# A transformer layer's residual stream moved into the output tensor by accumulating DMAs, its norm squares applied one sum later, and its down projection taken in three groups

## The chip, the cores and the metric

The kernel runs on one core of a Trainium2 chip. The metric is the device time of one execution in microseconds. The figure for a kernel is the median of its runs; beside it stands one profiled execution, whose trace is read here.

## What is computed

One layer of a streaming encoder on 640 tokens of width 2048 (512 of a prompt, 8 x 16 of samples). Only its second half matters here:

```python
merged = concatenate([rms_norm(attn, g_attn_out), rms_norm(ssm, g_ssm_out)])
h = x + merged @ w_out                                      # 2048 x 2048
f = rms_norm(h, g_ffn)
h = h + (silu(f @ w_gate) * (f @ w_up)) @ w_down            # 2048 x 5632, 5632 x 2048
gate = sigmoid(rms_norm(h, g_ple) @ w_ple_gate)             # 2048 x 2048
h = h + gate * (p_i @ w_ple_proj)
```

All in float32. The gate's other factor, `p_i @ w_ple_proj`, is computed earlier and lies in memory (`pj_dr`).

## The kernel before, in words

Activations are kept transposed: features on the partitions, tokens along the free axis, so a "pair" is two blocks of 128 features by 640 tokens (640 KB). After attention and the state-space part (up to about 780 us) come five stages of the same make: the output projection (cells `o`, 8 of them), the gate and up projections (`g` and `u`, 22 each), the down projection (`d`) and the gate for the layer input (`p`, 8). A cell multiplies weights by activations into one pair of output features. It does so by a Strassen-Winograd scheme: seven products of half-size blocks instead of eight, each into a PSUM bank of its own.

**Weight units.** A cell eats "units" of 512 KB: weights of 512 input features by 256 output features. `Ring` streams them: `load` (L53) has SP fetch a unit, two ahead; `split` (L67) has DVE form four sums (L109 to L112), ACT round the seven blocks to the short form (`wh`, L86) and DVE take the remainder (`wl`, L87). There are two buffers of each. A unit is 42 matmuls: seven products, two blocks of 128 input features, three terms (L1231 to L1233: high by high, high by low, low by high).

**Activation tiles.** The input of a stage stands in SBUF as tiles of 1120 KB a pair: the seven Winograd blocks. They are written to memory in that form (`fc_dr`, `tc_dr`, `hc_dr`; `keep`, L1193), fetched by SP (`fetch`, L1205) into one of eight places, and cut in two halves in place (`whole`, `cut`, L1075: ACT rounds, L1076; DVE subtracts, L1077). `fetch` issues the cut right behind the load, but for a few tiles that `cut_late` handles.

**A cell's end.** `strassen` (L1252) empties the seven banks: two copies on ACT (L1258, L1260), six adds on DVE (L1259 to L1265), one on POOL (L1266). Buffers for pairs rotate over two (`pair`, L1169).

**Behind an `o` cell** (L1303 to L1317): SP loads the pair of `x`; DVE adds it (L1306); ACT scales by the norm's weight into `c` (L1293); DVE forms the Winograd sums of `c` (L118 to L121); SP stores `c` and stores the sum to `h_dr` (L1316); ACT squares (L1275) and DVE adds the squares to the running sum (L1279, L1280). The norm's factor itself is applied behind the next stage's products (`by_rows`, L1282), once `scale_rows` has made it from the sum of squares.

**The down projection** has 44 blocks of 128 input features, that is 22 tiles or 11 units, for each of the 8 pairs of output, and only eight places. So `down_cells` (L129) visits each pair several times with some of the units: two groups of four pairs, 28 visits. A visit that isn't the last sends its sum to `h_dr` by an accumulating DMA from POOL (L1372). At the last visit SP loads what has been gathered (`hx`), DVE adds it (L1376), and scaling, Winograd sums, squares follow as above; the sum goes to `h2_dr`.

**The last stage** multiplies the sigmoid by `pj`, loads the pair of `h2_dr` (`hy`), adds it on POOL (L1399) and stores the output by SP (L1400). Its eighth cell is written out by hand so that little is left behind the last matmul.

The order of the instructions on each engine is not that of the text: a planner that the program uses at build time lays them out, with the text's order as preference. Each engine then goes through its own list in order.

Of the kernel before, what the change touches and what calls it, by code (L numbers as in the profile page):

```python
# [9 lines left out]
F32 = mybir.dt.float32  # L10
# [4 lines left out]
OP = mybir.AluOpType  # L15
# [113 lines left out]
def down_cells():  # L129

    low, high = range(4), range(4, 8)
    steps = [(low, 0, 2), (high, 0, 4), (low, 2, 6), (high, 4, 8), (low, 6, 8), (high, 8, 11), (low, 8, 11)]
    return [(j, range(a, b), a == 0, b == FT // 4) for js, a, b in steps for j in js]

# [28 lines left out]
def hybrid_step(ctx: ExitStack, tc: tile.TileContext, io):  # L165
# [21 lines left out]
    cells = down_cells()  # L187
    units += [(1, io["w_down"][j, u]) for j, us, _, _ in cells for u in us]
    units += [(1, io["w_pg"][j, u]) for j in range(8) for u in (2, 3, 0, 1)]
    ring = Ring(nc, stp, units)  # L190
# [5 lines left out]
    m_dr = dp.tile([D, NTOK], F32, name="m_dr")  # L196
    h_dr = dp.tile([D, NTOK], F32, name="h_dr")
    h2_dr = dp.tile([D, NTOK], F32, name="h2_dr")
    tc_dr = dp.tile([FT // 2, P, 7, NH2], F32, name="tc_dr")
# [732 lines left out]
    def attention(h):  # L932
# [133 lines left out]
    def scale_group(s, name):  # L1066
# [3 lines left out]
                  gp_.tile([P, NTOK], F32, tag="sq", name="rz" + name, bufs=2))  # L1070

    def rows(dram, j):
        return dram[2 * j * P : 2 * (j + 1) * P, :].rearrange("(a p) n -> p a n", p=P)

# [127 lines left out]

    later = {}

    def fetch(name, slot, dram, i, late=False):  # L1205
        k = kp_tile("k" + name, slot)
        x = k[:, 1].bitcast(F32)
        nc.sync.dma_start(x, dram[i])
        if late:
            later.setdefault(i // 2 - 2, []).append(lambda: whole(k, x))  # L1210
            return k
        return whole(k, x)

    def cut_late(u):
        for f in later.pop(u, ()):
            with tc.issue_after(ring.done[0]), tc.issue_after(ring.done[1]):
                f()

    def products(name, kps, after=None, order=None):
# [53 lines left out]

    def squares(s, x, t, first, other=nc.vector):
        nc.scalar.activation(t, x, AF.Square)  # L1275
        if first:
            nc.vector.tensor_tensor(s, t[:, 0], t[:, 1], op=OP.add)
        else:
            nc.vector.tensor_tensor(s, s, t[:, 0], op=OP.add)  # L1279
            other.tensor_tensor(s, s, t[:, 1], op=OP.add)  # L1280

# [12 lines left out]

    fk = []
    for j in range(8):
        after = None
        if j == 7:
            def after(u):
                for i in (2 * u, 2 * u + 1):  # L1300
                    if i < 7:
                        fk.append(fetch(f"f{i}", i, fc_dr, i, late=i == 6))
        r = strassen(f"o{j}", mk, after)  # L1303
        x = pair(f"x{j}")
        nc.sync.dma_start(x, io["xT"][2 * j : 2 * j + 2].rearrange("a p n -> p a n"))
        nc.vector.tensor_tensor(r, r, x, op=OP.add)  # L1306
        c = seven(f"c{j}")
        scaled(c, r, gffn, j)
        if j < 7:
            keep(nc.vector, c, fc_dr, j)  # L1310
        else:
            winograd_rows(nc.vector, c[:, :4], c[:, 4:])
            kf7 = kp_tile("kf7", 7)
            fk.append(kf7)
            later.setdefault(1, []).append(lambda: whole(kf7, c))
        nc.sync.dma_start(rows(h_dr, j), r)  # L1316
        squares(ssqh, r, x, j == 0)  # L1317

# [9 lines left out]
    for f in range(FT // 2):  # L1328
        z = strassen(f"g{f}", fk, cut_late if f == 0 else None)
# [18 lines left out]
    for j, us, _, _ in cells:  # L1348
        for u in us:
            uses[u] = uses.get(u, 0) + 1  # L1350
    hk, hslot = {}, {4: 6, 5: 7, 6: 0, 7: 1, 0: 2, 1: 3, 2: 4, 3: 5}
    ready = []

    def next_h():
        i = ready.pop(0)
        hk[i] = fetch(f"h{i}", hslot[i], hc_dr, i)

    for n, (j, us, first, last) in enumerate(cells):
        def after(i, us=us, n=n):
            uses[us[i]] -= 1  # L1360
            if not uses[us[i]] and n < len(cells) - 4:
                next_t()
            if n < 2 and i:
                next_t()
            if n == len(cells) - 1:
                for _ in range(min(2, 3 - i)):
                    if ready:
                        next_h()
# [7 lines left out]
        nc.vector.tensor_tensor(r, r, x, op=OP.add)  # L1376
        c = seven(f"hc{j}")
        scaled(c, r, gple, j)
        if j in (3, 4, 5):
            winograd_rows(nc.vector, c[:, :4], c[:, 4:])  # L1380
            hk[j] = whole(kp_tile(f"kh{j}", hslot[j]), c)
        else:
            keep(nc.vector, c, hc_dr, j)
            ready.append(j)
        nc.sync.dma_start(rows(h2_dr, j), r)
        squares(ssqp, r, x, j == 4)
    hk = [hk[i] for i in (4, 5, 6, 7, 0, 1, 2, 3)]
    for j in range(7):
        z = strassen(f"p{j}", hk)
        if j == 0:  # L1390
# [14 lines left out]
    nc.sync.dma_start(x, rows(pj_dr, 7))  # L1405
    nc.sync.dma_start(y, rows(h2_dr, 7))
    ps = products("p7", hk, order=(1, 2, 6, 5, 3, 7, 4))
# [145 lines left out]
```

## Time and profile before

| | |
|---|---|
| median of 3 runs | 2935.68 us (2934.81 to 2939.37) |
| the profiled execution, its own time | 2942.17 us |
| its span, first to last instruction | 2940.4 us |
| granted TensorE clock, mean | 0.984 |
| PE busy | 2828.1 us (96%) |
| DVE busy | 2241.3 us (76%) |
| ACT busy | 1241.2 us (42%) |
| POOL busy | 360.3 us (12%) |
| DMA | 449.16 MB, mean 153 GB/s |

PE is TensorE, DVE VectorE, ACT ScalarE, POOL GpSimd, SP SyncE. A wait is put down to the instruction that ended it. Busy time of PE is from the start of a matmul to its modelled end; matmuls overlap, so the count of matmuls in a stretch says more than the busy share.

### The profile page before, as it was taken

What the parts mean: (1) busy time and instruction counts of PE and PEld (TensorE: products, weight loads), DVE (VectorE), ACT (ScalarE), POOL (GpSimd) and SP (SyncE); (2) the same over time, 40 slices, a digit from 0 to 9 for tenths busy, and PEclk for the clock granted to TensorE, in tenths of its full rate; (3) what the DMA queues carried; (4) which work ended last, traced back from release to release, by engine and by line L of the source; (5) the groups of instructions that cost most, each with busy time, mean ns of one, the idle gap of its engine ahead of it and who ended that gap; (6) DMA issues with size and microseconds to landing.
All of it is one profiled execution on the core that took longest, in us unless ns stands there. A gap on an engine that the chain in (4) does not pass through costs nothing. (4 is left out here: it accounts for less than half of the span.)

```text
span 2940.4 us, 47366 instructions
## 1 busy us (share of the span) xinstructions
PE 2828.1 (96%) x19051; PEld 2716.3 (92%) x19051; DVE 2241.3 (76%) x3629; ACT 1241.2 (42%) x1628; POOL 360.3 (12%) x405
## 2 busy tenths in 40 slices
PE   8999999999889889999999999999999999999998
PEld 6889988887789889999999999999999999998898
DVE  7758254445688888888888888888887777899888
ACT  5343355556644453333333333333433344345433
POOL 1213300001000001101111111111110110100011
PEclk9999999999999999999999999999999999999999
DMA  5666734546545623232323333333555455647444
GB/s 174 168 187 179 244 118 169 182 156 239 205 141 180 240 98 125 95 124 96 119 101 118 102 118 102 118 102 118 205 145 148 135 158 170 164 158 273 136 158 140
DMA packets 137484, 449.16 MB, mean 153 GB/s; under 512 B 14096, under 2 KB 34672, under 8 KB 124464
## 3 DMA queue, kind: packets, MB, share of 16 engines
q1 hardware_dynamic: 120032, 396.47, 39.9%
q0 software_dynamic: 15936, 45.47, 6.1%
q10 hardware_dynamic: 1296, 4.20, 0.4%
q8 instruction: 149, 2.44, 0.3%
q14 instruction: 71, 0.58, 0.1%
HBM read 342.25 MB, written 101.18 MB: 151 GB/s over the span
## 5 line engine op out<-in xcount | busy, mean ns | idle before, releaser
L86 ACT ACTIVATE wh<-wst 128x768 fp32r<-128x768 f32 x328 | 276.9, 845 | 660.0 <-issue 320.0
L87 DVE TENSOR_TENSOR wl<-ws,wh 128x1024 fp32r<-128x1024 f32 x328 | 423.6, 1291 | 102.1 <-ACT wh L86 101.7
L86 ACT ACTIVATE wh<-ws 128x1024 fp32r<-128x1024 f32 x328 | 344.6, 1051 | 358.0 <-DVE ws L112 357.9
L87 DVE TENSOR_TENSOR wl<-wst,wh 128x768 fp32r<-128x768 f32 x328 | 334.3, 1019 | 169.8 <-ACT wh L86 169.7
L1231 PE MATMUL d<-kt,wh 128*128 128x320 f32 x1232 | 383.5, 315 | 11.7 <-ACT wh L86 5.4
L1231 PE MATMUL g<-kf,wh 128*128 128x320 f32 x1232 | 382.4, 311 | 5.5 <-ACT wh L86 5.3
L1232 PE MATMUL g<-kf,wh 128*128 128x320 f32 x1232 | 381.8, 310 | 0.0
L1232 PE MATMUL d<-kt,wh 128*128 128x320 f32 x1232 | 380.6, 312 | 0.0
L1231 PE MATMUL u<-kf,wh 128*128 128x320 f32 x1232 | 380.1, 309 | 0.0
L1233 PE MATMUL g<-kf,wl 128*128 128x320 f32 x1232 | 375.7, 310 | 4.5 <-DVE wl L87 4.5
L1232 PE MATMUL u<-kf,wh 128*128 128x320 f32 x1232 | 380.0, 309 | 0.0
L1233 PE MATMUL u<-kf,wl 128*128 128x320 f32 x1232 | 376.2, 309 | 0.1
L1233 PE MATMUL d<-kt,wl 128*128 128x320 f32 x1232 | 344.5, 315 | 7.3 <-DVE wl L87 7.3
L1231 PEld LDWEIGHTS d<-kt,wh 128*128 128x128 f32 x1232 | 234.9, 191 | 17.9 <-ACT wh L86 10.2
L1231 PEld LDWEIGHTS g<-kf,wh 128*128 128x128 f32 x1232 | 232.7, 189 | 6.8 <-ACT wh L86 6.8
L1233 PEld LDWEIGHTS g<-kf,wl 128*128 128x128 f32 x1232 | 230.3, 188 | 5.6 <-DVE wl L87 5.3
L1232 PEld LDWEIGHTS d<-kt,wh 128*128 128x128 f32 x1232 | 235.0, 191 | 0.0
L1233 PEld LDWEIGHTS d<-kt,wl 128*128 128x128 f32 x1232 | 224.7, 191 | 11.1 <-DVE wl L87 10.6
L1232 PEld LDWEIGHTS g<-kf,wh 128*128 128x128 f32 x1232 | 232.9, 189 | 0.0
L1231 PEld LDWEIGHTS u<-kf,wh 128*128 128x128 f32 x1232 | 231.3, 188 | 0.0
L1232 PEld LDWEIGHTS u<-kf,wh 128*128 128x128 f32 x1232 | 231.3, 188 | 0.0
L1233 PEld LDWEIGHTS u<-kf,wl 128*128 128x128 f32 x1232 | 230.2, 188 | 0.4 <-DVE wl L87 0.4
(488 smaller groups left out, 5878.4 us busy)
## 6 DMA issues: line engine op xcount, KB each, us to landing
wst<-in_w_gate SPq DMA_DIRECT2D x88, 512.0 KB
wst<-in_w_up SPq DMA_DIRECT2D x88, 512.0 KB
wst<-in_w_down SPq DMA_DIRECT2D x88, 512.0 KB
tc_dr<-t SPq DMA_DIRECT2D x22, 1120.0 KB
kt<-tc_dr SPq DMA_DIRECT2D x22, 1120.0 KB
wst<-in_w_qk SPq DMA_DIRECT2D x32, 512.0 KB
kc<-in_cache_k SPq DMA_DIRECT2D x16, 1024.0 KB
vc<-in_cache_v SPq DMA_DIRECT2D x16, 1024.0 KB
```

What stands on the lines that cost most here:

```text
L86: a = nc.scalar.activation(wh[:, part], x, AF.Copy)
L87: b = nc.vector.tensor_tensor(wl[:, part], x, wh[:, part].bitcast(F32), op=OP.subtract)
L1231: nc.tensor.matmul(ps[i], wh[:, a, w], k[:, 0, b], start=f, stop=False)
L1232: nc.tensor.matmul(ps[i], wh[:, a, w], k[:, 1, b], start=False, stop=False)
L1233: nc.tensor.matmul(ps[i], wl[:, a, w], k[:, 0, b], start=False, stop=l)
```

## The change

The sum `x + merged @ w_out` and all that is added to it later is gathered in the output tensor `o_yT` (its last pair in a small tensor `h7_dr`). During attention POOL issues seven copies of `x` into `o_yT`, from memory to memory. An `o` cell's result is added there by an accumulating DMA from POOL, and the sum is loaded back, also by POOL (`add_h`); scaling, Winograd sums and squares are done on the loaded pair one cell later (`done_o`). Only the last `o` cell adds `x` on DVE as before. The last visits of the down projection are treated in the same way (`done_h`), but for the very last. The last stage adds its product to `o_yT` by an accumulating DMA; the load of `hy` and POOL's add go.

Fetches of tiles move from SP to POOL, and a tile is no longer cut at the fetch: `cut_next` cuts a given number of tiles behind a unit, if they were fetched at least so many units ago; what is still uncut is cut ahead of its use. The down projection goes in three groups of two, three and three pairs, 26 visits. Two more tiles stay in SBUF instead of going through memory (cell 6 of `o`; pair 4 of the down projection's end), and the last stage takes its units in another order.

```diff
 def down_cells():
-    low, high = range(4), range(4, 8)
-    steps = [(low, 0, 2), (high, 0, 4), (low, 2, 6), (high, 4, 8), (low, 6, 8), (high, 8, 11), (low, 8, 11)]
+    one, two, three = (4, 5), (0, 1, 6), (7, 2, 3)
+    steps = [(one, 0, 2), (two, 0, 3), (three, 0, 4), (one, 2, 6), (two, 3, 7), (three, 4, 8), (one, 6, 8),
+             (two, 7, 11), (three, 8, 11), (one, 8, 11)]
...
     for h in range(H):
+        if h:
+            nc.gpsimd.dma_start(io["o_yT"][2 * (h - 1) * P : 2 * h * P, :].rearrange("(a p) n -> a p n", p=P), xrow(h - 1))
...
-    def fetch(name, slot, dram, i, late=False):
+    def fetch(name, slot, dram, i, eng=nc.gpsimd):
         k = kp_tile("k" + name, slot)
         x = k[:, 1].bitcast(F32)
-        nc.sync.dma_start(x, dram[i])
...
+        eng.dma_start(x, dram[i])
+        return wait_cut(k, x)
+
+    def cut_next(n=1, age=2):
+
+        for key in list(uncut)[:n]:
+            if tick[0] - uncut[key][0] >= age:
+                uncut.pop(key)[1]()
...
+    def add_h(r, j):
+
+        nc.gpsimd.dma_start(hrow(j), r, accum_op=OP.add)
+        x = pair(f"h{j}")
+        nc.gpsimd.dma_start(x, hrow(j))
+        return x
...
+    def done_o(x, j):
         c = seven(f"c{j}")
-        scaled(c, r, gffn, j)
-        if j < 7:
+        scaled(c, x, gffn, j)
+        if j < 6:
             keep(nc.vector, c, fc_dr, j)
         else:
             winograd_rows(nc.vector, c[:, :4], c[:, 4:])
...
+            f6.append(c)
+        squares(ssqh, x, j == 0)
+
+    for j in range(8):
+        def after(u, j=j):
+            if j == 7:
+                if u == 2:
+                    due.pop()()
...
+                for i in (2 * u, 2 * u + 1):
+                    if i < 6:
+                        fk.append(fetch(f"f{i}", i, fc_dr, i))
+                cut_next(2 if u == 2 else 1, 1)
+
+        r = strassen(f"o{j}", mk, after)
+        if j < 7 and due:
+            due.pop()()
+        if j < 7:
+            x = add_h(r, j)
+            due.append(lambda x=x, j=j: done_o(x, j))
+    fk.append(whole(kp_tile("kf6", 6), f6[0]))
+    x = due.pop()
+    nc.vector.tensor_tensor(x, x, r, op=OP.add)
...
             def after(u):
-                if u < 2:
+                if u < 3:
                     next_t()
+                cut_next((0, 0, 2, 1)[u], 1)
...
+            if end:
+                if i == 2:
+                    due.append(pair("h5"))
+                    nc.sync.dma_start(due[0], hrow(5))
+                for k in ((0, 1), (2, 3), ())[i]:
+                    next_h(k)
+            cut_next(1, 1 if n < 2 else 2)
 
         r = strassen(f"d{n}", [tk[i] for u in us for i in (2 * u, 2 * u + 1)], after)
         if not last:
-            nc.gpsimd.dma_start(rows(h_dr, j), r, accum_op=OP.add)
-            continue
-        x = pair(f"hx{j}")
-        nc.sync.dma_start(x, rows(h_dr, j))
-        nc.vector.tensor_tensor(r, r, x, op=OP.add)
...
+            nc.gpsimd.dma_start(hrow(j), r, accum_op=OP.add)
+        elif not end:
+            if due:
+                due.pop()()
+            x = add_h(r, j)
+            due.append(lambda x=x, j=j: done_h(x, j))
...
         nc.vector.tensor_tensor(z, z, x, op=OP.mult)
-        x = pair(f"hy{j}")
-        nc.sync.dma_start(x, rows(h2_dr, j))
-        nc.gpsimd.tensor_tensor(z, z, x, op=OP.add)
-        nc.sync.dma_start(rows(io["o_yT"], j), z)
+        nc.gpsimd.dma_start(hrow(j), z, accum_op=OP.add)
```

## Rows read from the trace of the kernel before

**Rows 1.** Busy time by stage: window, length, then each engine's busy us (count).

```profile
core 0: us, PE busy (x) PEld busy (x) DVE busy (x) ACT busy (x) POOL busy (x), PEclk, DMA share, GB/s
843.80:1007.70 163.90, 155.93 (x1051) 153.96 (x1051) 138.95 (x233) 67.78 (x82) 5.25 (x6) 1.00 0.51 180
1007.70:1065.80 58.10, 44.39 (x258) 41.19 (x257) 50.19 (x72) 36.51 (x40) 0.87 (x1) 0.91 0.59 229
1065.80:2125.80 1060.00, 1059.86 (x7227) 1059.60 (x7226) 878.76 (x1363) 384.62 (x463) 133.29 (x127) 1.00 0.34 114
2125.80:2156.90 31.10, 25.04 (x128) 22.67 (x128) 30.82 (x40) 14.32 (x16) 9.17 (x6) 0.78 0.45 175
2156.90:2551.40 394.50, 388.56 (x2605) 386.52 (x2605) 304.79 (x511) 154.92 (x188) 46.62 (x39) 0.99 0.55 156
2551.40:2686.80 135.40, 128.43 (x843) 123.28 (x842) 124.58 (x208) 63.63 (x77) 6.99 (x7) 1.00 0.53 175
2686.80:2750.80 64.00, 52.51 (x300) 48.89 (x299) 55.22 (x84) 37.15 (x42) 3.78 (x2) 0.89 0.60 223
2750.80:2940.40 189.60, 176.29 (x1178) 172.42 (x1176) 163.53 (x240) 66.62 (x80) 27.74 (x14) 0.98 0.45 152
```

**Rows 2.** Timeline of PE, its last matmul: start, us, instruction.

```profile
2931.60 0.31 PE L1233 MATMUL p<-kh,wl 128*128 128x320 f32 x1
```

**Rows 3.** Groups by line, 843.8 to 1007.7 us: count, busy us, mean ns, idle before.

```profile
L87 DVE TENSOR_TENSOR wl<-ws,wh 128x1024 fp32r<-128x1024 f32 x25 | 33.3, 1333 | 12.4 <-ACT wh L86 12.4
...
L87 DVE TENSOR_TENSOR wl<-wst,wh 128x768 fp32r<-128x768 f32 x25 | 24.5, 978 | 2.5 <-ACT wh L86 2.5
...
L109 DVE TENSOR_TENSOR ws<-wst 128x256 f32<-128x256 f32 x25 | 10.5, 419 | 0.2
...
L1306 DVE TENSOR_TENSOR ro<-ro,x 128x1280 f32<-128x1280 f32 x7 | 10.4, 1480 | 0.0
...
L1280 DVE TENSOR_TENSOR ssqa<-ssqa,x 128x640 f32<-128x640 f32 x6 | 4.9, 819 | 0.0
...
L119 DVE TENSOR_TENSOR c<-c 128x320 f32<-128x320 f32 x7 | 3.5, 493 | 1.5 <-ACT c L1293 1.4
...
L1259 DVE TENSOR_TENSOR ro<-qo,o 128x320 f32<-128x320 f32 x6 | 2.9, 480 | 0.0
```

**Rows 4.** Groups by line, 2156.9 to 2551.4 us: the cuts on DVE.

```profile
L1077 DVE TENSOR_TENSOR kt<-kt 128x1280 fp32r<-128x1280 f32 x13 | 19.3, 1486 | 8.9 <-ACT kt L1076 8.9
...
L1077 DVE TENSOR_TENSOR kt<-kt 128x960 fp32r<-128x960 f32 x12 | 13.8, 1151 | 0.0
```

**Rows 5.** Line L1372, the accumulating DMAs: duration of issue, ns, and landing.

```profile
L1372 POOL DMA_DIRECT2D h_dr<-rd x20: 1181/1190/1294, 2157.4 to 2550.9; - x20
...
DMA to landing us min/median/max: 6.6/7.8/14.4
```

**Rows 6.** Waits, 843.8 to 1007.7 us: total us, times, longest.

```profile
PE o L1231 <- ACT wh L86: 8.0, 6, 1.3
```

**Rows 7.** Timeline of ACT at the end of one cell: start, us, instruction, idle before.

```profile
974.22 1.55 ACT L1293 ACTIVATE c<-ro,c_g_ffn 128x640 f32<-128x640 f32 x2 [5.28 <-DVE ro L1306]
975.68 1.25 ACT L1275 ACTIVATE x<-ro 128x1280 f32<-128x1280 f32 x1
976.84 0.83 ACT L86 ACTIVATE wh<-wst 128x768 fp32r<-128x768 f32 x1
```

**Rows 8.** Waits, 2113 to 2760 us: ACT for tiles that are landing.

```profile
ACT kt L1076 <- DMA kt<-tc_dr: 22.7, 9, 4.9
...
ACT kh L1076 <- DMA kh<-hc_dr: 8.2, 3, 3.3
```

**Rows 9.** Groups by line of POOL, whole span: the add of the last stage.

```profile
L1399 POOL TENSOR_TENSOR rp<-rp,hy 128x1280 f32<-128x1280 f32 x7 | 21.6, 3089 | 80.9 <-DMA hy<-h_dr 80.9
```

**Rows 10.** Groups by line of DVE, 2750.8 to 2940.4 us.

```profile
L87 DVE TENSOR_TENSOR wl<-ws,wh 128x1024 fp32r<-128x1024 f32 x28 | 51.8, 1849 | 15.8 <-ACT wh L86 15.8
```

**Rows 11.** Busy time in the attention stretch, columns as in the first group.

```profile
376.00:780.00 404.00, 393.90 (x2886) 341.31 (x2885) 204.33 (x324) 235.10 (x352) 31.60 (x46) 1.00 0.50 177
```

More of the change, by code (lines that the diff above doesn't have):

```diff
@@ L187, in hybrid_step @@
     cells = down_cells()
-    units += [(1, io["w_down"][j, u]) for j, us, _, _ in cells for u in us]
-    units += [(1, io["w_pg"][j, u]) for j in range(8) for u in (2, 3, 0, 1)]
+    units += [(1, io["w_down"][j, u]) for j, us, _ in cells for u in us]
+    units += [(1, io["w_pg"][j, u]) for j in range(8) for u in (3, 0, 1, 2)]
     ring = Ring(nc, stp, units)
@@ L1201, in whole, with wait_cut @@
         return k
-    later = {}
-    def fetch(name, slot, dram, i, late=False):
+    uncut, tick = {}, [0]
+    def wait_cut(k, x):
+        uncut[id(k)] = tick[0], lambda: whole(k, x)
+        return k
+    def fetch(name, slot, dram, i, eng=nc.gpsimd):
         k = kp_tile("k" + name, slot)
         x = k[:, 1].bitcast(F32)
-        nc.sync.dma_start(x, dram[i])
[L1209 to L1217, printed above, removed]
+        eng.dma_start(x, dram[i])
[4 more added lines that the diff above has]
+                uncut.pop(key)[1]()
     def products(name, kps, after=None, order=None):
@@ L1272, in scale_rows, with squares @@
         row_scale(s, n, pm, y[:, 0], y[:, 1])
-    def squares(s, x, t, first, other=nc.vector):
-        nc.scalar.activation(t, x, AF.Square)
+    def squares(s, x, first):
+        nc.scalar.activation(x, x, AF.Square)
         if first:
-            nc.vector.tensor_tensor(s, t[:, 0], t[:, 1], op=OP.add)
+            nc.vector.tensor_tensor(s, x[:, 0], x[:, 1], op=OP.add)
         else:
-            nc.vector.tensor_tensor(s, s, t[:, 0], op=OP.add)
-            other.tensor_tensor(s, s, t[:, 1], op=OP.add)
+            nc.vector.tensor_tensor(s, s, x[:, 0], op=OP.add)
+            nc.vector.tensor_tensor(s, s, x[:, 1], op=OP.add)
+    def add_h(r, j):
[3 more added lines that the diff above has]
+        return x
     def by_rows(x, s):
@@ L1293, in scaled @@
             nc.scalar.activation(c[:, 2 * a : 2 * a + 2], halves(x[:, a]), AF.Copy, scale=gain[:, 2 * j + a : 2 * j + a + 1])
[L1295 to L1305, printed above, removed]
-        nc.vector.tensor_tensor(r, r, x, op=OP.add)
+    fk, due, f6 = [], [], []
+    def done_o(x, j):
         c = seven(f"c{j}")
-        scaled(c, r, gffn, j)
-        if j < 7:
+        scaled(c, x, gffn, j)
+        if j < 6:
             keep(nc.vector, c, fc_dr, j)
@@ L1312, in hybrid_step, with after_g0 @@
             winograd_rows(nc.vector, c[:, :4], c[:, 4:])
[L1313 to L1317, printed above, removed]
+            f6.append(c)
[5 more added lines that the diff above has]
+                    due.pop()()
+                    due.append(pair("x7"))
+                    nc.sync.dma_start(due[0], xrow(7).rearrange("a p n -> p a n"))
+                for i in (2 * u, 2 * u + 1):
[11 more added lines that the diff above has]
+    nc.vector.tensor_tensor(x, x, r, op=OP.add)
+    c = seven("c7")
+    scaled(c, x, gffn, 7)
+    nc.gpsimd.dma_start(hrow(7), x)
+    winograd_rows(nc.vector, c[:, :4], c[:, 4:])
+    fk.append(wait_cut(kp_tile("kf7", 7), c))
+    def after_g0(u, x=x):
+        if u == 1:
+            squares(ssqh, x, False)
+        cut_next(1, 0)
     tk, slots = {}, (0, 1, 2, 3, 4, 5, 6, 7)
@@ L1347, in hybrid_step @@
     uses = {}
-    for j, us, _, _ in cells:
+    for j, us, _ in cells:
         for u in us:
             uses[u] = uses.get(u, 0) + 1
[L1351 to L1359, printed above, removed]
+    hk, hslot = {}, {6: 6, 7: 7, 0: 0, 1: 1, 2: 2, 3: 3, 4: 4, 5: 5}
+    due, h4 = [], []
@@ new lines, in done_h, with next_h, after @@
+    def done_h(x, j):
+        c = seven(f"hc{j}")
+        scaled(c, x, gple, j)
+        if j in (6, 7, 4):
+            winograd_rows(nc.vector, c[:, :4], c[:, 4:])
+            if j == 4:
+                h4.append(c)
+            else:
+                hk[j] = wait_cut(kp_tile(f"kh{j}", hslot[j]), c)
+        else:
+            keep(nc.vector, c, hc_dr, j)
+        squares(ssqp, x, j == 0)
+    def next_h(j):
+        hk[j] = fetch(f"h{j}", hslot[j], hc_dr, j)
+    for n, (j, us, last) in enumerate(cells):
+        end = n == len(cells) - 1
+        def after(i, us=us, n=n, end=end):
+            if end and i == 2:
+                due.pop()()
@@ L1360, in after @@
             uses[us[i]] -= 1
-            if not uses[us[i]] and n < len(cells) - 4:
+            if not uses[us[i]] and us[-1] < FT // 4 - 1:
                 next_t()
-            if n < 2 and i:
+            if n == 0 and not i:
                 next_t()
[L1365 to L1368, printed above, removed]
+            if end:
[4 more added lines that the diff above has]
+                    next_h(k)
@@ L1385, in hybrid_step @@
-        nc.sync.dma_start(rows(h2_dr, j), r)
-        squares(ssqp, r, x, j == 4)
-    hk = [hk[i] for i in (4, 5, 6, 7, 0, 1, 2, 3)]
+            nc.gpsimd.dma_start(hrow(j), r, accum_op=OP.add)
+        elif not end:
+            if due:
+                due.pop()()
+            x = add_h(r, j)
+            due.append(lambda x=x, j=j: done_h(x, j))
+    hk[4] = whole(kp_tile("kh4", hslot[4]), h4[0])
+    x = due.pop()
+    nc.vector.tensor_tensor(x, x, r, op=OP.add)
+    c = seven("hc5")
+    scaled(c, x, gple, 5)
@@ L1388, in hybrid_step, with after_p0 @@
+    nc.gpsimd.dma_start(hrow(5), x)
+    winograd_rows(nc.vector, c[:, :4], c[:, 4:])
+    hk[5] = wait_cut(kp_tile("kh5", hslot[5]), c)
+    hk = [hk[i] for i in (6, 7, 0, 1, 2, 3, 4, 5)]
+    def after_p0(u, x=x):
+        if u == 1:
+            squares(ssqp, x, False)
+        cut_next(1, 0)
     for j in range(7):
-        z = strassen(f"p{j}", hk)
+        z = strassen(f"p{j}", hk, after_p0 if j == 0 else None)
         if j == 0:
@@ L1405, in hybrid_step @@
     nc.sync.dma_start(x, rows(pj_dr, 7))
-    nc.sync.dma_start(y, rows(h2_dr, 7))
+    nc.sync.dma_start(y, hrow(7))
     ps = products("p7", hk, order=(1, 2, 6, 5, 3, 7, 4))
```

28 lines of the change are left out of this document (13 added, 15 removed).

## The prediction

> **What bounds the kernel now.** The page first: TensorE is busy 96% of the span, with no one wait that could be taken away whole, so I asked stage by stage what its product loop costs beyond its undisturbed pace. The table of stages [rows 1] does that. The stage of the gate and up projections, 1065.8 to 2125.8 us, holds 172 weight units of 42 matmuls (7227 counted) in 1060.0 us with PE busy for 1059.86: 6.163 us for a unit. The change touches it only at its two edges, so this is the pace that the other stages are held to, and "excess" is a stage's length less 6.163 times its units (count of matmuls over 42):
> - output projection, second to last cell (843.8 to 1007.7): 163.9 - 25 x 6.163 = 9.8 us
> - its last two units and the first gate cell (1007.7 to 1065.8): 58.1 - 6 x 6.163 = 21.1
> - entry of the down projection (2125.8 to 2156.9): 31.1 - 3 x 6.163 = 12.6
> - its middle (2156.9 to 2551.4): 394.5 - 62 x 6.163 = 12.4
> - its last visits to each pair of rows (2551.4 to 2686.8): 135.4 - 20 x 6.163 = 12.1
> - its end and the first cell of the gate for the layer input (2686.8 to 2750.8): 64.0 - 7 x 6.163 = 20.9
> - the rest (2750.8 to 2940.4): 189.6 - 28 x 6.163 = 17.0, of which 8.5 lie behind the last matmul [rows 2].
>
> So at most 97 us can be touched. The same rows say what limits: DVE is busy 50.2 of 58.1, 30.8 of 31.1, 124.6 of 135.4 and 55.2 of 64.0 us at the edges and the last visits, but only 304.8 of 394.5 in the middle. At the edges DVE's work has to be spread or cut; in the middle it fits and is only bunched.
>
> What DVE does there has prices [rows 3, 4]. Preparing one weight unit: 1333 + 978 + 4 x 419 ns = 4.0 us. Emptying a cell: 6 x 480 ns = 2.9. The closing work of a row pair ("done"): the residual add 1.48, four winograd sums 4 x 0.49, two sums of squares 2 x 0.82, so 5.1. Cutting a tile of activations into its two halves: 1.486 + 1.151 = 2.6 us on DVE.
>
> **The change, part by part.**
>
> *Residual add by DMA.* It takes L1306 off seven cells and L1376 off seven: 14 x 1.48 us of DVE. A "done" then costs 3.6 us, and its inputs come from memory instead of from the same cell. In its place POOL issues an accumulating DMA and, when that has landed, a load. The nearest row, the accumulations that exist [rows 5], gives 1.19 us of issue and a landing at 7.8 us; a load of the same size is not timed, so I bound it between nothing and that landing: 9 to 17 us from the emptied cell to the loaded pair. The "done" now stands one cell later (18.5 us where a cell has three units, 24.7 where it has four), so it fits, by 1.5 us at worst. If it didn't, ACT, in whose queue the scaling stands, would hold up the weight copies behind it.
>
> *Order at the ends of cells in the output projection.* Six times PE waits there for the weight copy, 8.0 us in all [rows 6]. The cause is ACT's queue [rows 7]: it idles 5.28 us for the residual add, then does two scalings and a square, and only at 976.84 the copy that PE wants. With a pair that landed earlier, scalings and square fill the idle time. Between 0 and all 9.8 us; I take 7.
>
> *Edge to the gate cells.* The number of cuts is the same (eight); cell 6's "done" moves into the last cell. On DVE one 3.6 us "done" is added and one add of 1.48 goes: +2.1 us. What can be won is DVE's idle time, 58.1 - 50.2 = 7.9 us, now that cuts are placed one or two behind a unit instead of at the fetch. The fetches, though, go from SP to POOL, where the first pair stands behind the accumulation of cell 6. Bounds: 8 won to 8 lost; I take 3 won.
>
> *Entry of the down projection.* Again eight cuts, 8 x 2.6 = 21 us, now from two units before the stage to seven units later, one a unit: 4.0 + 2.6 = 6.6 us of DVE against 6.163 of PE, and the emptying of cells on top. So an excess stays: over seven units 7 x 0.45 + 2 x 2.9 = 9 us. 4 won, bounds 0 and 9.
>
> *Middle.* The excess is bunches of four cuts at the changes of group, and ACT standing before a cut whose tile hasn't landed: 22.7 us in nine waits for the tiles of the down projection and 8.2 in three for those of the last stage [rows 8]. With three groups a freed pair of tiles has four or more units before its use, and a cut waits two units after the fetch, 12.3 us, where the longest of these waits was 4.9. Two cells fewer save 2 x 2.9 us of DVE, where there is slack: nothing. Bounds 4 and 12; I take 9.5.
>
> *Last visits.* Before: three units a cell, DVE 3 x 4.0 + 2.9 + 5.1 = 20.0 us against 18.5 of PE, always behind. After: the first three cells have four units (16.0 + 2.9 + 3.6 = 22.5 against 24.7), the others 18.5 against 18.5, with two cuts among them. 7 won of 12.1; bounds 3 and 12.
>
> *Edge to the last stage.* Six cuts before and after; four tiles instead of five come back from memory. DVE's count: two dones of 3.6 and one of 5.1 (12.3) against two of 5.1 (10.2), so +2.1 us; against that DVE's idle 64.0 - 55.2 = 8.8 us and ACT's waits for tiles. 4 won; bounds 7 won and 5 lost.
>
> *Last stage.* POOL's add, 3089 ns seven times [rows 9], goes, with the load that fed it; an accumulation of 1.19 us issue takes its place. While that add runs, DVE's own work is slow: the second half of a weight unit takes 1849 ns there [rows 10] against 1333 in rows 3. Of the 8.5 us of excess ahead of the last matmul I take 5; bounds 0 and 8.
>
> *Copies of the input into the output* during attention: seven transfers of 640 KB from memory to memory, each one issue on POOL, which is busy 31.6 of 404 us there, with the DMA engines half busy and PE 393.9 of 404 [rows 11]. The trace has no such copy. From below nothing, and no gain either, as nothing there gets shorter; from above the landing of rows 5 reaching PE each time, 7 x 7.8 = 55 us. PE hardly waits in this stretch with transfers of 512 and 1024 KB going on all the time, so I take 0.
>
> Sum: 7 + 3 + 4 + 9.5 + 7 + 4 + 5 = 39.5 us. The profiled execution took 2942.2 us (span 2940.4); it becomes 2902.7. It lies 6.5 us above the median of the runs, 2935.7, so the median goes to 2896.
>
> One rule speaks against moving transfers to POOL. Rows 5 show the issue of POOL's accumulations at 1181 to 1294 ns over 20 of them, amid a busy DVE. The Trainium skill (SBUF — State Buffer, the opening section with its warning "The 'DVE blocks DMA' trap") says that GpSimd cannot write a DMA's descriptors while DVE holds the port pair that they share, and advises issuing from SP or ACT. By that rule a POOL issue would now and then take far longer than its neighbours; the spread of rows 5 does not bear that out, and the time by it is the third rival's.
>
> **Rivals.**
> 1. *Order was all of it.* If the reordering cures the edges too, two thirds of the 97 us go: 2936 - 65 = 2871. For it: DVE's idle time at both edges. Against: DVE's counts there, which hardly fall. 0.14.
> 2. *DVE stays the bound and the cuts only move.* Edges, entry and last visits win nothing, the middle half: 5 (output cells) + 5 + 4 = 14 us, 2922. For it: DVE busy 30.8 of 31.1 us at the entry. 0.12.
> 3. *POOL's queue becomes the wait (slower).* Each load of a pair stands on POOL behind the landing of its accumulation, and fetches stand behind the load; where the pair is late, ACT waits at the scaling and the weight copies behind it are late for PE. There are 14 such places; the case turns slower from 39.5 / 14 = 2.8 us of lateness at PE for each, and at 3.4 us gives 14 x 3.4 - 39.5 = +8: 2944. For it: landings of up to 14.4 us [rows 5] and a margin of 1.5 us. Against: the median of 7.8. The port rule of the Trainium skill, above, would act through the same place. 0.07.
> 4. *The change does not do what it says in time*: stalls go from one edge to the next, 2936 within 6. 0.05.
>
> **How the numbers follow.** Forecast 0.62, by itself 2880 to 2912 (the bounds of the parts rarely fall on one side together). Two runs of this kernel differ by about 0.2%, 6 us, so that is what "same" means. Faster: 0.62 + 0.14 + 0.11 of rival 2 = 0.87; same: 0.01 + 0.05 = 0.06; slower: 0.07. The range of 8 in 10 goes from rival 1's time to a little past rival 2's: 2869 to 2925; outside are rivals 3 and 4 and a part of the first.
>
> **What would show it.** Right: at the cell ends of the output projection ACT does scalings and square before the sum of its own cell ends, and PE's waits there fall under 3 us; the middle of the down projection comes within 4 us of 6.163 a unit; ACT's waits for landing tiles fall under 8 us; DVE's weight halves in the last stage fall to 1.3 us; the edges still have DVE busy over 85%, with 14 to 18 us of excess each at the edge to the gate and the edge to the last stage. Wrong: ACT waiting for the loaded pairs at their scaling, POOL's accumulations issued in over 2 us, new excess in the attention stretch beside the copies, or edges without excess.

## The result, and the profile after

The changed kernel takes 3008.52 us (median of 4 runs, 3006.25 to 3011.42) against 2936.30 (4 runs, 2934.81 to 2939.37): a ratio of 1.0245, interval 1.0227 to 1.0263. That is slower by 72 us, and 84 us above the top of the range. The profiled execution has a span of 3008.0 us (before 2940.4) and a mean granted clock of 0.968 (before 0.984).

The busy time by stage, columns and stages as in [rows 1]. Each stage begins at the same weight unit as there, except for the last visits: they begin four units earlier, at unit 269, as they do in the changed kernel.

```profile
core 0: us, PE busy (x) PEld busy (x) DVE busy (x) ACT busy (x) POOL busy (x), PEclk, DMA share, GB/s
858.00:1034.20 176.20, 162.85 (x1053) 159.38 (x1052) 124.18 (x223) 66.13 (x81) 19.32 (x21) 0.96 0.57 162
1034.20:1096.70 62.50, 45.38 (x258) 42.73 (x257) 51.29 (x73) 37.92 (x42) 9.43 (x7) 0.84 0.49 194
1096.70:2161.40 1064.70, 1062.04 (x7226) 1059.52 (x7225) 882.23 (x1365) 384.89 (x462) 135.84 (x133) 1.00 0.34 114
2161.40:2197.70 36.30, 26.92 (x128) 24.68 (x127) 33.59 (x44) 16.30 (x18) 9.89 (x9) 0.76 0.50 178
2197.70:2567.30 369.60, 363.96 (x2438) 361.51 (x2437) 280.46 (x469) 143.29 (x173) 44.71 (x46) 0.99 0.53 151
2567.30:2751.30 184.00, 162.49 (x1010) 156.32 (x1009) 129.03 (x221) 69.95 (x84) 20.28 (x20) 0.93 0.51 144
2751.30:2822.70 71.40, 51.17 (x300) 48.20 (x299) 57.50 (x90) 36.27 (x41) 7.50 (x9) 0.83 0.50 179
2822.70:3008.00 185.30, 174.81 (x1178) 172.40 (x1176) 147.60 (x240) 70.54 (x85) 14.41 (x14) 0.99 0.46 131
```

DVE is less busy in the output cells (124 against 139 us) and in the last stage (148 against 164), as the change meant it to be; yet the output cells take 12 us longer. The first window also starts 14 us later. With the prediction's measure, length less 6.163 us for each unit, all kernels of this study stand like this (us; e1 to e10 are the experiments below; "start" is where the first `o` matmul lies; the last visits begin at unit 269 in every row; the beginning of the `o` stage, five units with 22 to 23 us of excess in all of them, is left out). Each row is one execution; those of e2, e3 and e8 are the quickest of their runs, 6 to 8 us under the median.

| kernel | start | output cells | edge to gate | gate, up | entry | middle | last visits | last edge | last stage | span |
|---|---|---|---|---|---|---|---|---|---|---|
| before | 790.2 | 9.9 | 21.1 | −0.1 | 12.6 | 12.5 | 12.1 | 20.9 | 17.0 | 2940.4 |
| after | 804.7 | 22.1 | 25.6 | 4.7 | 17.8 | 12.1 | 36.1 | 28.2 | 12.7 | 3008.0 |
| e1 | 792.4 | 25.0 | 24.2 | 4.7 | 16.7 | 11.7 | 37.3 | 28.3 | 12.7 | 2996.8 |
| e2 | 799.0 | −0.1 | 25.1 | 0.5 | 12.8 | 11.2 | 13.8 | 29.1 | 10.8 | 2946.3 |
| e3 | 798.2 | 5.1 | 18.4 | 1.1 | 14.0 | 11.0 | 15.0 | 19.7 | 12.8 | 2939.5 |
| e4 | 803.6 | 22.6 | 21.5 | 3.3 | 12.1 | 9.1 | 30.4 | 26.6 | 13.3 | 2986.9 |
| e5 | 795.2 | −0.1 | 25.4 | 0.5 | 12.5 | 11.1 | 14.9 | 27.9 | 10.8 | 2942.7 |
| e6 | 786.4 | −0.1 | 20.0 | 8.6 | 6.1 | 11.6 | 17.6 | 26.5 | 11.3 | 2932.4 |
| e7 | 789.9 | −0.1 | 21.7 | 8.6 | 6.2 | 11.6 | 14.3 | 20.4 | 14.9 | 2931.7 |
| e8 | 785.9 | 9.9 | 20.7 | −0.5 | 12.7 | 12.1 | 11.7 | 19.4 | 10.6 | 2926.7 |
| e9 | 791.2 | 3.6 | 18.6 | 6.7 | 12.4 | 11.2 | 12.5 | 19.1 | 10.5 | 2930.5 |
| e10 | 790.7 | 3.5 | 18.2 | 3.1 | 12.5 | 11.9 | 11.9 | 20.3 | 8.9 | 2925.4 |

The loss sits in three places: the start (+14.4), the stages with a loaded pair (output cells +12.2, last visits +24.0) and the edges (+4.5, with +4.8 at the head of the gate stage behind it, +5.2, +7.3).

**The loaded pairs.** ACT's waits behind 790 us (total us, times, longest):

```profile
ACT c L1316 <- DMA h<-o_yT: 41.2, 7, 7.7
ACT kt L1085 <- DMA kt<-tc_dr: 35.4, 11, 6.9
...
ACT hc L1316 <- DMA h<-o_yT: 30.7, 6, 8.7
...
ACT hc L1316 <- DVE h L1445: 9.8, 1, 9.8
...
ACT hc L1316 <- DMA h<-h_dr: 4.6, 1, 4.6
```

The three lines on `c` and `hc` that end with a DMA are the 14 loaded pairs (the single one comes from `h7_dr`). Together they cost ACT 76.5 us: the two that are scaled inside a cell wait 1.2 and 0.3 us, each of the other twelve 4.6 to 8.7. One of these, on the timelines of POOL, ACT and PE (start, us, instruction, idle before):

```profile
884.85 1.20 POOL L1300 DMA_DIRECT2D o_yT<-ro  x1 [2.44 <-issue]
894.20 0.75 POOL L1302 DMA_DIRECT2D h<-o_yT  x1 [8.16 <-DMA o_yT<-ro]
...
898.60 1.55 ACT L1316 ACTIVATE c<-h,c_g_ffn 128x640 f32<-128x640 f32 x2 [7.73 <-DMA h<-o_yT]
900.06 0.83 ACT L86 ACTIVATE wh<-wst 128x768 fp32r<-128x768 f32 x1
...
903.88 0.44 ACT L1274 ACTIVATE qo<-o 128x320 f32<-128x320 f32 x1 [0.16 <-PE o L1245]
...
900.94 0.64 PE L1243 MATMUL o<-km,wh 128*128 128x320 f32 x1 [4.03 <-ACT wh L86]
```

The pair is back 13.7 us after the issue of its accumulation (884.85 to 898.60), within the 9 to 17 that the prediction gave it. But the scaling isn't where the text has it, behind the next cell's emptying (903.88): the planner put it ahead of that, and ACT stood 7.73 us in front of it with the weight copy of 900.06 behind. PE stood 4.03 us, and paid once more afterwards. The granted clock of PE in the same 8 us, columns as above:

```profile
898.00:900.00 2.00, 0.00 (x0) 0.00 (x0) 0.54 (x2) 1.40 (x2) 0.00 (x0) 1.00 0.01 3
900.00:902.00 2.00, 1.06 (x4) 1.03 (x4) 2.00 (x5) 2.00 (x4) 0.00 (x0) 0.53 0.00 0
902.00:904.00 2.00, 2.00 (x8) 1.65 (x7) 2.00 (x4) 1.84 (x4) 0.00 (x0) 0.50 0.35 39
904.00:906.00 2.00, 2.00 (x10) 2.00 (x9) 2.00 (x5) 0.32 (x1) 0.00 (x0) 0.50 0.97 331
```

A clock of 0.50 is the lower level, 1.2 GHz: from 902 us on 8 and 10 matmuls in 2 us, where the same view has 16 and 15 at 1.00 from 892 on. So of the excess of the output cells, 22.1 us, 13.4 are idle (176.2 − 162.85) and 8.8 are longer matmuls (162.85 less 25 × 6.163); in the last visits it is 21.5 and 14.6. In the cells of before, with waits of 1.3 us at most [rows 6], the clock is 1.00 [rows 1].

**The copies of the input.** The seven copies, by line: duration of issue in ns, first and last start in us:

```profile
L1047 POOL DMA_DIRECT2D o_yT<-in_xT x7: 486/486/530, 16.4 to 19.4; - x7
```

They were issued at 16 to 19 us, not during attention. The first 50 us of the kernel after:

```profile
0.00:50.00 50.00, 34.00 (x127) 25.45 (x128) 31.03 (x61) 26.16 (x36) 15.81 (x31) 0.90 0.88 305
```

and of the kernel before:

```profile
0.00:50.00 50.00, 41.58 (x155) 31.96 (x156) 37.03 (x70) 30.95 (x42) 12.46 (x24) 0.97 0.69 224
```

The DMA engines go from 69 to 88% busy just when the first activations and weights are wanted, and PE has 28 matmuls fewer behind it. On the timelines of ACT and PE there:

```profile
34.87 0.83 ACT L262 ACTIVATE a<-x,c_g_mix 128x640 fp32r<-128x640 f32 x1 [8.65 <-DMA x<-in_xT]
...
39.23 2.50 PE L514 MATMUL acc<-wh,a 128*128 128x512 f32 x5 [9.42 <-ACT wh L77]
```

**The last edge.** ACT and DVE around 2806 us, and a wait of PE from 2785 to 2815 us:

```profile
2796.49 0.41 ACT L1276 ACTIVATE rd<-d 128x320 f32<-128x320 f32 x1
2806.67 1.55 ACT L1316 ACTIVATE hc<-h,c_g_ple 128x640 f32<-128x640 f32 x2 [9.78 <-DVE h L1445]
2808.13 0.83 ACT L86 ACTIVATE wh<-wst 128x768 fp32r<-128x768 f32 x1
...
2805.09 1.49 DVE L1445 TENSOR_TENSOR h<-h,rd 128x1280 f32<-128x1280 f32 x1
...
PE p L1243 <- ACT wh L86: 11.6, 2, 10.6
```

It is the same fault with another source: the very last pair is still added on DVE, ACT stands 9.78 us before its scaling, and the weight copy behind it lets PE wait 10.6 us.

**The last stage** went as forecast: 17.0 to 12.7.

### The profile page after: what moved, and what is told of

Read it like the earlier page. It is cut to its first block, busy times and chain, and to the rows that moved or that the text cites. A ratio compares the mean times of both kernels' runs of the same rounds, so it can differ in the third digit from the quotient of the medians.

```text
span 3008.0 us, 47275 instructions
## 1 busy us (share of the span) xinstructions
PE 2857.0 (95%) x19051; PEld 2740.2 (91%) x19051; DVE 2198.5 (73%) x3603; ACT 1240.8 (41%) x1624; POOL 391.3 (13%) x470
## 5 line engine op out<-in xcount | busy, mean ns | idle before, releaser
L87 DVE TENSOR_TENSOR wl<-ws,wh 128x1024 fp32r<-128x1024 f32 x328 | 407.5, 1242 | 128.3 <-ACT wh L86 127.6
L1243 PE MATMUL d<-kt,wh 128*128 128x320 f32 x1232 | 389.4, 319 | 29.7 <-ACT wh L86 20.4
L1244 PE MATMUL d<-kt,wh 128*128 128x320 f32 x1232 | 386.2, 317 | 0.0
L1245 PE MATMUL u<-kf,wl 128*128 128x320 f32 x1232 | 368.7, 309 | 0.2 <-DVE wl L87 0.2
L1245 PE MATMUL d<-kt,wl 128*128 128x320 f32 x1232 | 351.4, 317 | 10.8 <-DVE wl L87 10.6
L1243 PEld LDWEIGHTS d<-kt,wh 128*128 128x128 f32 x1232 | 239.6, 195 | 36.8 <-ACT wh L86 25.2
L1243 PEld LDWEIGHTS g<-kf,wh 128*128 128x128 f32 x1232 | 233.3, 189 | 18.5 <-ACT wh L86 9.3
L1244 PEld LDWEIGHTS d<-kt,wh 128*128 128x128 f32 x1232 | 239.8, 195 | 0.0
```

What stands on the lines that cost most here:

```text
L87: b = nc.vector.tensor_tensor(wl[:, part], x, wh[:, part].bitcast(F32), op=OP.subtract)
L1243: nc.tensor.matmul(ps[i], wh[:, a, w], k[:, 0, b], start=f, stop=False)
L1244: nc.tensor.matmul(ps[i], wh[:, a, w], k[:, 1, b], start=False, stop=False)
L1245: nc.tensor.matmul(ps[i], wl[:, a, w], k[:, 0, b], start=False, stop=l)
```

## The experiments

Ratios are to the kernel before, with their intervals, from runs on the same chip. e1 to e4 each change one thing of the changed kernel.

**e1: the copies queued behind an instruction of the attention head before.**

```diff
+        behind[0] = nc.gpsimd.tensor_copy(diag, ...).ins
...
-            nc.gpsimd.dma_start(io["o_yT"][...], xrow(h - 1))
+            with tc.issue_after(behind[0]):
+                nc.gpsimd.dma_start(io["o_yT"][...], xrow(h - 1))
```

> The changed kernel, with each of the seven copies of the input into the output queued on POOL behind an instruction of the head before (the first behind a memset at the start of attention). Theory: the copies have nothing to wait for, were issued at 16.4 to 19.4 us and kept the first loads from landing; 12.9 of the 67.6 us between the two spans come from there. Then the first output cell starts within 2 us of 790.2 us, the rest is as in the changed kernel, and the time falls by 12 to 15 us, to about 2995. Rival: the late start has another cause (the order of the first stage, or the run), and the start stays at about 804 us. Second rival: the copies cost as much in attention, where the DMA engines are half busy, and the start is late by more than 5 us all the same.

Measured: 2998.97 us, 1.0207 (1.0190 to 1.0224). The copies by line:

```profile
L1048 POOL DMA_DIRECT2D o_yT<-in_xT x7: 498/509/524, 353.0 to 523.0; - x7
```

The output projection starts at 792.4 instead of 804.7. Over all kernels, with the copies first (after, e2, e3, e4) it starts at 801.4 on average, with them in attention (e1, e5, e6, e7, e9) at 791.0, without them (before, e8, e10) at 788.9, each kernel's start varying by some 4 us. The loss is made in the first 50 us: the matmul that starts at 50.0 us in the kernel before starts 7.9 to 9.9 us later in the four with the copies first, and 1.1 to 4.0 us earlier in the seven others. So the place of the copies cost some 10 us. In attention they cost about 2, which is inside the spread.

**e2: each "done" queued on ACT behind the next cell's emptying** (for the two that belong inside a cell: behind the weight copies issued so far).

```diff
-        nc.scalar.activation(r12, ps[3], AF.Copy)
+        emptied[0] = nc.scalar.activation(r12, ps[3], AF.Copy).ins
...
         if j < 7 and due:
-            due.pop()()
+            with tc.issue_after(emptied[0]):
+                due.pop()()
...
```

> The changed kernel, with the closing work on a loaded pair queued on ACT behind the emptying of the next cell (behind the last weight copy in the two places where it stands inside a cell). Theory: the build-time planner put the scaling into ACT's queue 6 to 8 us ahead of the landing of the pair (13 to 14 us from the issue of the accumulation), and the weight copies behind it were late; ACT's 72 us of waits for the pairs fall under 10 us, excess falls from 22.1 to about 6 in the output cells, from 36.1 to about 12 at the last visits and from 28.2 to about 20 at the edge to the last stage, so 40 to 50 us less in all, about 2963. Rival (DVE is full there, and the order on ACT only shows it): ACT's waits go, PE's excess stays within 10 us of what it was, 3000.

Measured: 2954.39 us, 1.0061 (1.0044 to 1.0078), 54 us less than the changed kernel for an order alone. ACT's waits for loaded pairs, from 780 us on:

```profile
ACT hc L1318 <- DMA h<-o_yT: 1.2, 1, 1.2
ACT c L1318 <- DMA h<-o_yT: 0.8, 2, 0.5
```

and the output cells by stage:

```profile
852.40:1006.40 154.00, 154.00 (x1052) 154.00 (x1051) 126.18 (x226) 67.10 (x80) 24.72 (x21) 1.00 0.64 188
```

76.5 us of waits became 2.0, and PE is busy all of the 154.0 us. Cells and last visits fall by 22.2 and 22.3 us, 44.5 in all, or 3.7 for each of the twelve pairs that are scaled there. The last edge stays (29.1): its wait for DVE's add was not touched (8.6 us in this run). Nor does the edge to the gate win (25.1): the pair of cell 6, issued among the fetches that POOL sends there, takes far longer than the others. POOL, and the times from issue to landing of the loads of pairs in this run (the longest is this one's):

```profile
1001.84 1.25 POOL L1302 DMA_DIRECT2D o_yT<-ro  x1
...
1019.79 0.72 POOL L1304 DMA_DIRECT2D h<-o_yT  x1 [6.13 <-DMA o_yT<-ro]
...
DMA to landing us min/median/max: 4.3/5.6/14.7
```

That is 32.7 us from the issue of the accumulation to the landed pair. ACT scales it at 1035.65 us, and the emptying for which PE stands 10.6 us follows on ACT only at 1043.57.

**e3: the add on DVE again** (SP loads `x` or the gathered pair, DVE adds, SP stores; the "done" still one cell later, its place left to the planner).

```diff
-        nc.gpsimd.dma_start(hrow(j), r, accum_op=OP.add)
         x = pair(f"h{j}")
-        nc.gpsimd.dma_start(x, hrow(j))
+        nc.sync.dma_start(x, src)
+        nc.vector.tensor_tensor(x, x, r, op=OP.add)
+        nc.sync.dma_start(hrow(j), x)
```

> The changed kernel with the sum formed on DVE again: SP loads the input pair (at the last visits the gathered pair), DVE adds, SP stores; the closing work still comes one cell later, groups, cuts and fetches as in the changed kernel. Theory (the round trip through memory is what ACT waits for): excess of the output cells, last visits and last edge falls as far as in the run with the work queued behind, less the 14 adds of 1.48 us, so 25 to 40 us less, 2970 to 2983. Rival (DVE is the bound): with 14 x 1.48 us more on DVE the time is no less than 3000.

Measured: 2949.72 us, 1.0038 (1.0025 to 1.0051), 20 us under the expected range. ACT still stands before its scalings, now for DVE's add. ACT's waits for added pairs behind 780 us (output cells, then last visits), and PE's in the output cells:

```profile
ACT c L1317 <- DVE h L1302: 31.8, 6, 5.4
ACT hc L1317 <- DVE h L1302: 17.2, 7, 5.3
...
PE o L1243 <- ACT wh L86: 1.3, 6, 0.3
```

So the planner puts the scaling ahead of its pair here too; but ACT's waits are shorter, 49.0 us against 76.5, and PE's waits for the weight copy in the output cells, 10.6 us in the change, fall to 1.3. The edge to the gate, with no pair to come back from memory, falls to 18.4. The add by DMA, the heart of the change, was a loss as laid out, and 14 × 1.48 us of DVE handed back cost less than it.

**e4: fetches on SP again** (the default of `fetch`'s argument `eng` is `nc.sync` in place of `nc.gpsimd`).

> The changed kernel with the tiles fetched by SP as before (the four of the last edge, six of the edge to the gate cells and the 22 of the down projection). Theory: on POOL they land in 8.5 us (down projection) and 11.5 to 13.9 us (the edges) and ACT waits 35.4 us for them; on SP they land earlier, ACT's waits for tiles halve, and the edge to the gate cells, the entry and the middle win 3 to 5 us each, about 10 us in all, 2998. Rival: the lateness is the landing itself and the transfers that run beside it, whichever queue issues them: no difference beyond 4 us, or worse, since weights stand behind them on SP again.

Measured: 2990.16 us, 1.0175 (1.0159 to 1.0191). The edge to the gate, the entry, the middle and the last visits each win 3 to 6 us, though ACT's waits for tiles of the down projection only fall from 35.4 to 25.3 us. POOL's queue as the fetches' place cost some 18 us. The pairs' waits are no smaller (85.4 us).

**e5: e1 and e2 together.**

> The changed kernel with both repairs: copies queued in attention and closing work queued behind the next cell's emptying. Theory (two separate causes that add up): 10 us from the copies (span 3008.0 to 2996.8 alone) and 54 to 62 us from the queue of ACT (median 3008.5 to 2954.4 alone) give a median of about 2942 to 2946, within 0.4% of the kernel before; then what is left of the change is worth nothing in sum. Rival (they overlap, a late start being made good later): no better than 2952.

Measured: 2940.78 us, 1.0009 (0.9999 to 1.0019): the change without these two misplacements is worth nothing.

**e6: e5, fetches on SP, and each cut of `cut_next` queued behind the weight copies issued so far.**

```diff
-                uncut.pop(key)[1]()
+                with tc.issue_after(ring.done[0]), tc.issue_after(ring.done[1]):
+                    uncut.pop(key)[1]()
```

> Both repairs, tiles fetched by SP, and each cut queued on ACT and DVE behind the last weight preparation traced before it. Theory: ACT's waits for tiles (32.4 us with the closing work queued behind) come from cuts placed ahead of the landing as well; with cuts queued back they fall under 15 us, the middle of the down projection falls from 11.2 to under 7 us of excess and the entry from 12.8 to about 9, so about 8 to 12 us below the run with both repairs, 2930 to 2936. Rival (DVE's bunches are the middle's cost, not ACT's waits): ACT's waits fall and the excess of the middle stays at 10 or more.

Measured: 2935.44 us, 0.9991 (0.9982 to 1.0000). ACT no longer waits for any tile of the down projection, and the entry falls from 12.5 to 6.1. The middle seems to stay, at 11.6, but its excess now lies elsewhere. Its first four units, and the 54 units behind them (columns as above):

```profile
2144.30:2177.30 33.00, 28.54 (x170) 25.94 (x168) 27.11 (x41) 14.65 (x17) 3.28 (x3) 0.95 0.45 104
2177.30:2513.30 336.00, 334.89 (x2270) 332.63 (x2269) 263.88 (x436) 136.28 (x162) 34.43 (x30) 1.00 0.53 157
```

The first four, next to the entry, have 8.4 us of excess, where all other kernels but e7 have none. The 54 with the changes of group have 3.2, against 12.5 in before and 11.1 in e5. So the entry's cuts moved in part over the border of the two stages, and most of the excess of the middle proper went; entry and middle together are at 17.7, against 23.6 in e5 and 25.1 in before. At the other end 8.6 us appear at the start of the gate stage, 5.9 of them in its first unit behind the edge: there the cuts only moved.

**e7: e6, but the last visits add on DVE** as in e3, their "done" left to the planner.

> As the run with all work queued back and fetches on SP, but at the last visits of the down projection the gathered sum is loaded by SP and added on DVE again; the output cells keep the accumulating DMA. Theory: the round trip is worth its price where it has a cell of four units (output cells: excess -0.1 with the work queued behind) and costs at the edge to the last stage (29.1 with the round trip against 19.7 with the add on DVE); so the edge falls to about 20 and the whole is 5 to 9 us below the run before it, about 2925. Rival (seven adds of 1.48 us on a full DVE outweigh it): last visits and edge together no lower than with the round trip.

Measured: 2929.34 us, 0.9969 (0.9959 to 0.9980). The last edge falls from 26.5 to 20.4. The only wait of ACT for a scaling that is left at that edge:

```profile
ACT hc L1328 <- DMA hc_dr<-hc: 2.5, 1, 2.5
```

In e6 it still stood 9.4 us for DVE's add of the last pair; with that wait gone the edge is back at before's level, and no lower.

**e8: the kernel before, with only the last stage by accumulating DMA.**

```diff
-        x = pair(f"hy{j}")
-        nc.sync.dma_start(x, rows(h2_dr, j))
-        nc.gpsimd.tensor_tensor(z, z, x, op=OP.add)
-        nc.sync.dma_start(rows(io["o_yT"], j), z)
+        nc.gpsimd.dma_start(rows(io["o_yT"], j), z, accum_op=OP.add)
```

> The kernel before with one part of the change: the sum of the down projection is stored into the output (its last pair where it was), and the last stage adds to it by an accumulating DMA from POOL; the load and POOL's add go. Theory: POOL's add of 3.09 us slowed DVE's weight halves to 1849 ns; without it they come to about 1250 ns and the last stage's excess falls from 17.0 to 11 to 13, 4 to 6 us less in all, about 2932. Rival (the stage has slack for it): less than 2 us.

Measured: 2935.33 us, 0.9989 (0.9980 to 0.9998), last stage 17.0 to 10.6. DVE there:

```profile
L87 DVE TENSOR_TENSOR wl<-ws,wh 128x1024 fp32r<-128x1024 f32 x28 | 36.8, 1314 | 15.8 <-ACT wh L86 15.8
```

That is 1849 ns with POOL's add beside it [rows 10], 1314 without: the part does what was forecast, alone as well.

**e9: the kernel before, with the output cells 0 to 5 added by DMA (copies in attention, "done" queued as in e2) and the last stage as in e8.**

> The kernel before with two parts of the change alone: output cells 0 to 5 add by DMA (copies queued in attention) with their closing work queued behind the next cell's emptying, and the last stage adds by DMA. Groups, fetches, cuts and last visits are those of before. Theory (these two parts hold all that the change can win; three groups and spread cuts only move DVE's bunches): excess of the output cells falls from 9.9 to 0 to 2, of the last stage from 17.0 to about 11, the rest stays within 2 us a stage: 14 to 17 us below the kernel before, ratio 0.9945 to 0.9955, below the run with the add on DVE at the last visits (0.9969). Rival (three groups and spread cuts are worth something after all): ratio no lower than 0.9969.

Measured: 2930.50 us, 0.9971 (0.9960 to 0.9983): less than expected, and at the mark that was set for the rival. The output cells keep 3.6 us, with one wait of 8.1 us left on ACT for a loaded pair. Three groups with queued cuts do win in one place: entry and middle are at 23.6 us together here, and at 17.8 in e7. But e7 loses nearly as much at the edge to the gate and in the gate stage behind it, 30.3 us against 25.3.

**e10: e9, but cells 0 to 5 add on DVE**: SP loads `x`, DVE adds, SP stores, no copies and no round trip; the "done" one cell later and queued.

```diff
-            nc.gpsimd.dma_start(hrow(j), r, accum_op=OP.add)
             x = pair(f"x{j}")
-            nc.gpsimd.dma_start(x, hrow(j))
+            nc.sync.dma_start(x, io["xT"][...])
+            nc.vector.tensor_tensor(x, x, r, op=OP.add)
+            nc.sync.dma_start(hrow(j), x)
```

> As the run before it, but the input pair is loaded by SP and added on DVE in output cells 0 to 5 (no copies, no accumulation there); the closing work is queued one cell later all the same. Theory (what PE waited for was the order on ACT, the scaling standing ahead of the weight copy, and not the 1.48 us of DVE): the output cells' excess is 0 to 3, within 2 us of the run with the DMA. Rival (the add's time on DVE counts in a stage where DVE is busy 139 of 164 us): 5 us or more of excess, about 6 x 1.48 us above the run with the DMA.

Measured: 2927.32 us, 0.9957 (0.9944 to 0.9969): 0.4% less than the kernel before, and the lowest median of all. PE's waits in the output cells:

```profile
PE o L1233 <- ACT wh L86: 1.8, 3, 0.8
```

8.0 us [rows 6] have become 1.8 with DVE's add kept, and the cells are at 3.5, as in e9. It was the order on ACT that held PE there, not the 1.48 us of the add.

## Why the prediction was wrong

It forecast 40 us won, and 72 were lost. The third rival named the wait and had 0.07.

**The step that failed first** is "The 'done' now stands one cell later (18.5 us ...), so it fits, by 1.5 us at worst." It took the place of the scaling from the text, though the planner lays out each engine's list and the text is only its preference. The round trip was about as long as bounded (11.8 to 17.2 us over the 14 pairs, against 9 to 17), and the scaling stood too early; e2, which changes nothing else, takes the waits from 76.5 to 2.0 us and 54 us off the time. The third rival's price was near: it had 14 × 3.4 = 47.6 us, and 44.5 came back in e2, 3.7 for each of twelve pairs. Its reason, POOL's queue, holds for the fetches (e4) and not for the pairs, whose waits are no smaller with the fetches on SP. What it set against them, the 39.5 us of gains, is what did not come.

**The copies**: "Copies of the input into the output *during attention* ... so I take 0" failed in the same way. They depend on nothing, so they went to the head of POOL's list, where they cost 10 us (e1); in attention, where the step costed them, about 2, inside the spread.

The terms of the sum, each with its measure (the orders mended, e2 to e7):
- *Output cells*, 7 forecast: 10.0 (e2), all of the excess. Right in kind.
- *Last stage*, 5 forecast: 4.3 in the change, 6.4 alone (e8). Right.
- *Middle*, 9.5 forecast: 0.4 (after) to 1.5 (e3), and 3.4 with fetches on SP alone (e4). The step "a cut waits two units after the fetch" failed like the first: in the text it does, in the engines' lists it stood where the planner put it. ACT still waits 35.4 us for tiles of the down projection (22.7 in before [rows 8]), and the cuts still come in bunches. DVE and PE at a change of group, and the clock behind it:

```profile
2539.49 2.55 DVE L1086 TENSOR_TENSOR kt<-kt 128x1280 fp32r<-128x1280 f32 x2
2541.96 0.48 DVE L1277 TENSOR_TENSOR qd<-qd,d 128x320 f32<-128x320 f32 x1
...
2542.49 0.64 PE L1243 MATMUL d<-kt,wh 128*128 128x320 f32 x1 [1.73 <-DVE qd L1277]
...
2543.00:2545.00 2.00, 2.00 (x8) 1.64 (x7) 2.00 (x4) 0.00 (x0) 2.00 (x1) 0.50 0.03 8
```

  A tile's cut, two instructions, stands on DVE ahead of the emptying of a bank that PE wants; PE waits 1.73 us and goes on at the lower clock. Of before's 12.5 us, 12.6 lie in three units (4.6, 4.0 and 4.0), with a wait for the same add (L1261 of before) in each; of after's, 11.1 in two (5.2 and 5.9). Fewer places, each dearer. In e6, with the cuts tied behind the weights, ACT waits for no such tile, and the 54 units behind the entry's spill hold 3.2 us: 9.3 of 12.5 gone, near the forecast. Whether the tiles' landing or the bunches made that difference was not separated.
- *Entry*, 4 forecast: 0.2 lost with the order of "done" mended (e2). In e6 it is 6.4 lower than in e5, but 8.4 lie in the four units behind it: moved, not won.
- *Last visits*, 7 forecast: 1.7 lost (e2), 2.2 (e7). The step took DVE's count (20.0 against 18.5 us of PE) as the bound; the add of 1.48 us off DVE did not pay, and with it back (e3, e7) the stage is within 1.5 us of e2's.
- *Edges*, 3 and 4 forecast: 4 and 8 lost (e2). Of the second, the wait for DVE's add of the last pair is 8.6; without it (e3, e7) it is 0.5 to 1.2 better than before. The first is 2.7 better than before where no pair comes back from memory (e3); in e2 the pair of cell 6 needs 32.7 us, beyond the bound of 17, and in e6 the cuts go from one side of the edge to the other. That DVE stays the bound there, the second rival, fits the little that was won but is not shown: in the change DVE is busy 82 and 81% of the two edges, under the 85% that the prediction named, and the longest wait of PE shown, 10.6 us, is for a copy on ACT.
- *Fetches moved to POOL*, which the prediction priced only at the first edge: about 18 us over four stages (e4).

Right, then: the order on ACT, POOL's add beside DVE, and, but for the pairs among the edges' fetches, the time of the round trip. POOL's accumulations from the down projection were issued in 1178 to 1240 ns, from the last stage in 1176 to 1217. The rule of the Trainium skill that was weighed (SBUF — State Buffer, section "SBUF: two separate sides", the warning on the "DVE blocks DMA" trap) is stated for DVE operations in a 2-port mode, a condition that the prediction left out. The trace does not bear the rule out here; whether any instruction of DVE beside these issues was in that mode, no run shows.

## What to carry to other kernels

Where a planner lays out the queues, the distance between two steps in the text is no margin: an instruction that waits for a slow source (a DMA's round trip, a loaded engine) must be tied behind the work that is to run first, or it may stand, as here, at the head of an in-order engine with everything behind it. The same holds for a transfer that depends on nothing: here it went out first, when it made the DMA engines 88% busy. Before handing an add to a DMA to relieve an engine, try the reordering alone; here that won no less (e10 against e9). What the cuts tied behind the weights win at the middle (e6, e7) was not tried together with e10.

## What the runs showed that had not been expected

- A wait of PE costs more than itself. After standing 4.03 us it ran at the lower level, 0.50, to about 907 us, with 0.267 us from one matmul to the next instead of 0.147; the 21 matmuls from 900.94 to 907.02 took 6.1 us, and at 0.147 they take 3.1. The length of one wait does not tell whether this follows. The waits of 1.3 us at most in the cells of before were not followed by a stretch at that level, but 1.73 us with 0.67 before it were, and in the kernel before, at a change of group, 1.04 us with 0.58 behind it:

```profile
2393.89 0.41 PE L1231 MATMUL d<-kt,wh 128*128 128x320 f32 x1 [1.04 <-DVE qd L1261]
...
2395.02 0.44 PE L1233 MATMUL d<-kt,wl 128*128 128x320 f32 x1 [0.58 <-DVE wl L87]
...
2396.00:2398.00 2.00, 2.00 (x9) 2.00 (x9) 2.00 (x6) 0.00 (x0) 0.56 (x1) 0.50 0.00 0
```

- Seven copies of 640 KB, memory to memory, cost 10 us at the start, with the DMA engines 88% busy over 50 us, and about 2 us, inside the spread, in attention, where they are half busy [rows 11].
